# One-hot gate spreading with per-partition scalars, and expert low parts on one engine, in a one-core transformer layer

## The chip, the cores and the metric

The kernel runs on one core of a Trainium2 chip. The metric is device time in microseconds of one execution, median of several. Three runs of the kernel before took 3920.32, 3934.92 and 3938.32 us; its profiled execution took 3923.52 us.

## The reference

One layer of a latent-token backbone works on 512 tokens of width 2048: a mixer (state-space scan, pooling, gated merge, output projection), and then the part that the change touches, a product-key expert layer:

```
q = (h @ w_q) -> 8 heads, two halves of 128
s1, s2 = q half @ k1, k2                 # 128 scores each
top 16 of s1, top 16 of s2, top 16 of the 256 sums -> expert id = i1*128 + i2
g = softmax(top scores)                   # 128 (head, expert) pairs per token
act = gelu(h . u_tab[expert]) * g
out = sum over the pairs of act * v_tab[expert]     # 16384 experts of 2048
```

Afterwards comes the residual with a gate and a final normalization. All is float32.

## The kernel before

The expert layer begins after the mixers. It treats the first 128 tokens (tile 0) by gathering: for each of 128 (head, expert) pairs it fetches the rows of both tables by an indirect DMA from GpSimd (line 1081), takes the dot product on VectorE (line 1096), the gelu on ScalarE (1097, 1098), and adds the scaled row of the second table on VectorE (1089). The other 384 tokens (tiles 1 to 3) are done densely: `dense_u` multiplies them with the whole first table, `dense_v` with the whole second one, with the gates spread into a dense token-by-expert matrix.

TensorE reads float32 as a high and a low part, three products for one (lines 110 to 112). So each half MB of a table that is loaded (`wload`, line 124; 256 loads in `dense_u`, 256 in `dense_v`) is cast to its high part `whi` by ScalarE (125), and the low part `wlo = wraw - whi` is subtracted by VectorE or GpSimd (126). `lo_eng` deals these subtractions out: an accumulator grows by `lo_pool` = 0.5 at each load and gives the work to GpSimd whenever it reaches 1, so every other one. There are three buffers each for raw, high and low parts. `last_lo` is the latest subtraction recorded on VectorE.

Beside the loads run two lanes, stepped by `tick` in every `wload`: lane 0 is the gathering of tile 0 (0.29 pairs a load, later 0.25), lane 1 (1.1 steps a load) the preparation `prep`: `picks` turns the sorted keys of a tile into indices and softmax gates (lines 1043 to 1065, among them six VectorE operations over 128x2048), `dense_keys` transposes them so that the 128 pairs lie on the partitions, and `dense_gates` spreads them. For each group of four tokens, `dense_gates` makes one-hot matrices of the two key indices (line 1144, two operations), multiplies the second by the three bfloat16 pieces of the gate (1146, one operation over 3x4x128), and TensorE multiplies them (1152, twelve matmuls) into the gates of these tokens, which ScalarE copies out (1153). There are 96 such groups, so 192 steps of lane 1; they run between about 1725 and 2550 us.

A scheduler orders the instructions of each engine from its own estimate of times; subtractions and casts have a high priority. GpSimd's order is that of the code. `issue_after(last_lo)` queues the VectorE instructions of a block behind the last recorded subtraction; of the parts here only the gathering's are so bound. In `dense_v`, each four rows of gate products are multiplied by GpSimd (1199, `sr`), cast by ScalarE (135, `ah`) and subtracted on VectorE (136, `al`).

Of the kernel before, what the change touches and what calls it, by code (L numbers as in the profile page):

```python
# [6 lines left out]
F32 = mybir.dt.float32  # L7
F32R = mybir.dt.float32r
BF16 = mybir.dt.bfloat16
# [3 lines left out]
OP = mybir.AluOpType  # L13
# [4 lines left out]
P = 128  # L18
# [75 lines left out]
class Builder:  # L94
# [1018 lines left out]
    def dense_keys(self, t, res, ix):  # L1113

        nc, V, kp = self.nc, self.nc.vector, self.keep
        ps = self.psT.tile([P, 512], F32, tag="tr", name=self.nm("pst"))
        for j, x in enumerate(res[t]):
            nc.tensor.transpose(ps[:, j * P:(j + 1) * P], x, self.ident)
        iT = kp.tile([P, 2, P], BF16, name=self.nm("iT"))
        nc.scalar.copy(iT, ps[:, 0:2 * P].rearrange("p (j t) -> p j t", j=2))  # L1120
        wb = kp.tile([P, 3, P], BF16, name=self.nm("wb"))
        wf = self.tq.tile([P, P], F32, tag="wf", name=self.nm("wf"))
        r = self.tq.tile([P, P], F32, tag="wr", name=self.nm("wr"))
        V.tensor_copy(r, ps[:, 2 * P:3 * P])
        for q in range(3):
            V.tensor_copy(wb[:, q], r)
            if q < 2:
                V.tensor_copy(wf, wb[:, q])
                V.tensor_tensor(r, r, wf, op=OP.subtract)
        ix[t] = (iT, wb)  # L1130
        yield

    def dense_gates(self, ix):

        nc, V, NT = self.nc, self.nc.vector, 4
        for j, t in enumerate(DT):
            iT, wb = ix[t]
            for tg in range(P // TG):
                st = self.stp.tile([P, P, TG], F32, tag="ast", name=self.nm("ast"))
                for t4 in range(TG // NT):  # L1140
                    ts = slice(tg * TG + t4 * NT, tg * TG + t4 * NT + NT)
                    oh = self.ohp.tile([P, 2, NT, P], BF16, tag="oh", name=self.nm("oh"))
                    for q in range(2):
                        V.tensor_tensor(oh[:, q], self.io4, iT[:, q, ts].unsqueeze(2).broadcast_to([P, NT, P]), op=OP.is_equal)  # L1144
                    R = self.ohp.tile([P, 3, NT, P], BF16, tag="R", name=self.nm("R"))
                    V.tensor_tensor(R, oh[:, 1].unsqueeze(1).broadcast_to([P, 3, NT, P]),
                                    wb[:, :, ts].unsqueeze(3).broadcast_to([P, 3, NT, P]), op=OP.mult)
                    yield
                    ps = self.psT.tile([P, 512], F32, tag="tr", name=self.nm("psd"))
                    for n in range(NT):  # L1150
                        for q in range(3):
                            nc.tensor.matmul(ps[:, n * P:(n + 1) * P], oh[:, 0, n, :], R[:, q, n, :], start=(q == 0), stop=(q == 2))  # L1152
                    nc.scalar.copy(st[:, :, t4 * NT:t4 * NT + NT], ps.rearrange("p (t e) -> p e t", t=NT))
                    yield
                nc.scalar.dma_start(self.Gd[:, j * (P // TG) + tg], st)
# [103 lines left out]
    def peer(self):  # L1259
        tc, nc, I = self.tc, self.nc, self.I  # L1260
        pool = lambda **k: tc.tile_pool(**k)
        self.Sd = [self.dram.tile([P, NC, ND * P], F32, name=f"sd{c}") for c in range(P // NC)]
        self.Gd = self.dram.tile([P, ND * P // TG, P, TG], F32, name="gds")
        with self.es() as es:
            en = es.enter_context
            en(tc.manual_schedule(engines={mybir.EngineType.Pool}))
            ap = en(pool(name="ffn", bufs=1))
            acc0 = ap.tile([P, D], F32, name="ffn0")
            self.sm = sm = en(pool(name="sm3", bufs=4))
            es_k = self.es()  # L1270
            en = es_k.enter_context
            more = en(pool(name="wlo2", bufs=1))
            self.wlo = Turns([self.wlo, self.wlo, more])
            self.keep = en(pool(name="keep", bufs=1))
            self.rowp = en(pool(name="rows2", bufs=3))
            es_u = self.es()
            self.tq = es_u.enter_context(pool(name="tq", bufs=1))
            self.ohp = es_u.enter_context(pool(name="oh", bufs=2))
            self.io4 = self.tq.tile([P, 4, P], BF16, name="io4")
            nc.vector.tensor_copy(self.io4, self.iota.unsqueeze(1).broadcast_to([P, 4, P]))  # L1280
            res, ix = {}, {}

            def prep():
                yield from self.picks(self.tkp, 0, res)
                self.lane0[2].append(self.gather_tile(0, res, acc0))
                for t in DT:
                    yield from self.picks(self.tkp, t, res)
                    yield from self.dense_keys(t, res, ix)
                self.es_t.close()
                self.stp = es_u.enter_context(pool(name="ast", bufs=1))  # L1290
                yield from self.dense_gates(ix)

            self.lane0 = lane0 = self.lane(0.29, [])
            lane1 = self.lane(1.1, [prep()])
            self.lo_acc, self.lo_pool = 0.0, 0.5
            es_v = self.es()
            self.raw, self.A = {}, {}

            def late():
# [12 lines left out]
            for x in (self.ahp, self.alp):  # L1312
                x.pools += [pa] * 3
            op = es.enter_context(pool(name="outs", bufs=1, side="right"))
            outs = [op.tile([P, D], F32, name=f"ffn{t}") for t in DT]
            fp = es_v.enter_context(pool(name="fin", bufs=1))
            self.g2 = self.brow(fp, self.modd[:, 3 * D:4 * D], "g2b")
            self.fw = self.brow(fp, I["final_w"], "fwb")
            self.ss = [fp.tile([P, 4], F32, name=f"ssf{j}") for j in range(TT)]
            lane0[0], self.lo_pool = 0.25, 0.5  # L1320
            self.dense_v(outs)
            self.drain(lane0)
            es_v.close()
            es_k.close()
        self.hp.close()
# [70 lines left out]
```

## Time and profile before

| what | us or share |
|---|---|
| three runs | 3920.32, 3934.92, 3938.32 |
| profiled execution, and its span from first to last instruction | 3923.52, 3921.8 |
| granted TensorE clock over the span | 0.98 |
| busy: PE, DVE, ACT, POOL | 94%, 70%, 30%, 47% |
| `dense_u`: first and last matmul | 1593.1 to 2809.4 |
| `dense_v`: first and last matmul | about 2811 to 3904 |

PE is TensorE, DVE is VectorE, ACT is ScalarE, POOL is GpSimd. Matmuls are pipelined, so the duration of one is longer than the time from its start to the next one's start. Short VectorE instructions overlap in the same way: one starts before the end that is recorded for the one in front of it. The busy time of VectorE and GpSimd includes whatever holds an instruction up once it has started.

### The profile page before, as it was taken

The page shows a single profiled execution, that of the slowest core. Times are in us where ns is not written, and L with a number is a line of the kernel's source. Part 1 is how long each engine was busy: PE and PEld are TensorE (multiplying, and loading weights), DVE is VectorE, ACT ScalarE, POOL GpSimd, SP SyncE. Part 2 cuts the span into 40 slices and gives each one's busy share as a digit, 9 for nine tenths or more (in the row PEclk, how much of TensorE's full clock was granted, in tenths as well). Part 3 has the DMA queues.
Part 4 walks back from the last instruction along what each step waited for, and adds up shares of the span by engine and source line. Part 5 has one row for each costly group of instructions (what it writes and reads, how often), then busy time and mean ns, then how long its engine had stood idle before and what let it go on. Part 6 is the DMA issues. An engine that isn't in the chain of part 4 may idle for free. (4 is left out here: it accounts for less than half of the span.)

```text
span 3921.8 us, 49308 instructions
## 1 busy us (share of the span) xinstructions
PE 3686.4 (94%) x18841; PEld 3128.2 (80%) x18841; DVE 2732.1 (70%) x3331; ACT 1178.3 (30%) x1752; POOL 1834.7 (47%) x997
## 2 busy tenths in 40 slices
PE   5999998879899989899999999999999999999997
PEld 2478876657777868799999999999877878878886
DVE  4364369997473268999999999965666665666564
ACT  3223331112232232233333333333332333333232
POOL 0043115553223223355555655555565776676652
PEclk8999999999999999999999999999999999999999
DMA  8635658879876422378878878788887988888773
GB/s 263 213 118 182 213 165 231 225 218 289 245 235 199 135 75 91 105 248 285 299 282 300 301 286 300 278 300 296 320 301 258 321 298 286 304 298 298 273 278 120
DMA packets 456381, 954.40 MB, mean 243 GB/s; under 512 B 104720, under 2 KB 248464, under 8 KB 421072
## 3 DMA queue, kind: packets, MB, share of 16 engines
q1 hardware_dynamic: 380320, 584.58, 46.6%
q0 software_dynamic: 46464, 301.03, 21.0%
q10 hardware_dynamic: 29360, 65.64, 4.5%
q8 instruction: 147, 2.41, 0.2%
q14 instruction: 90, 0.74, 0.1%
HBM read 859.88 MB, written 94.93 MB: 243 GB/s over the span
## 5 line engine op out<-in xcount | busy, mean ns | idle before, releaser
L125 ACT CAST whi<-wraw 128x1024 fp32r<-128x1024 f32 x712 | 746.4, 1050 | 1724.9 <-PE psU L111 307.3
L126 POOL TENSOR_TENSOR wlo<-wraw,whi 128x1024 fp32r<-128x1024 f32 x284 | 792.5, 2791 | 803.6 <-ACT whi L125 591.6
L126 DVE TENSOR_TENSOR wlo<-wraw,whi 128x1024 fp32r<-128x1024 f32 x428 | 621.2, 1451 | 560.1 <-ACT whi L125 309.4
L112 PE MATMUL psU<-h2Th,wlo 128*128 128x384 f32 x2048 | 696.8, 340 | 42.5 <-DVE wlo L126 26.0
L110 PE MATMUL psU<-h2Th,whi 128*128 128x384 f32 x2048 | 702.0, 343 | 5.2 <-ACT whi L125 5.1
L111 PE MATMUL psU<-h2Tl,whi 128*128 128x384 f32 x2048 | 694.3, 339 | 0.0
L111 PE MATMUL psV<-wlo,ah 128*128 128x512 f32 x1536 | 607.0, 395 | 12.9 <-POOL wlo L126 7.1
L112 PE MATMUL psV<-whi,al 128*128 128x512 f32 x1536 | 605.9, 394 | 0.0
L110 PE MATMUL psV<-whi,ah 128*128 128x512 f32 x1536 | 556.1, 395 | 4.3 <-DVE ffn L1231 4.3
L112 PEld LDWEIGHTS psU<-h2Th,wlo 128*128 128x128 f32 x2048 | 388.8, 190 | 50.9 <-DVE wlo L126 19.3
L1096 DVE SCALAR_TENSOR_TENSOR row<-row,h 128x2048 f32<-128x2048 f32 x128 | 352.3, 2752 | 81.8 <-DMA row<-in_u,eid 81.7
L110 PEld LDWEIGHTS psU<-h2Th,whi 128*128 128x128 f32 x2048 | 388.6, 190 | 7.3 <-ACT whi L125 7.1
L111 PEld LDWEIGHTS psU<-h2Tl,whi 128*128 128x128 f32 x2048 | 389.0, 190 | 0.0
L1089 DVE SCALAR_TENSOR_TENSOR ffn<-row,w,ffn 128x2048 f32<-128x2048 f32 x127 | 351.3, 2766 | 18.0 <-DMA row<-in_v,eid 17.9
L111 PEld LDWEIGHTS psV<-wlo,ah 128*128 128x128 f32 x1536 | 290.1, 189 | 85.5 <-POOL wlo L126 11.7
L1081 POOL DMA_INDIRECT row<-in_u,eid x128 | 221.4, 1730 | 269.4 <-ACT w L1097 132.5
L110 PEld LDWEIGHTS psV<-whi,ah 128*128 128x128 f32 x1536 | 289.7, 189 | 71.1 <-issue 4.7
L112 PEld LDWEIGHTS psV<-whi,al 128*128 128x128 f32 x1536 | 289.5, 189 | 67.0
L1081 POOL DMA_INDIRECT row<-in_v,eid x128 | 277.0, 2164 | 20.0 <-issue 9.2
L819 DVE SCALAR_TENSOR_TENSOR lacc<-lw,sil,lacc 128x512 f32<-128x512 f32 x240 | 213.7, 891 | 58.6 <-DMA lw<-in_w_mod 56.5
L112 PE MATMUL psg<-hhi,wlo 128*128 128x512 f32 x512 | 203.1, 401 | 25.9 <-DVE wlo L126 25.8
L1144 DVE TENSOR_TENSOR oh<-io,iT 128x512 bf16<-128x512 bf16 x192 | 211.6, 1141 | 6.3 <-PE psd L1152 6.2
(349 smaller groups left out, 5567.4 us busy)
## 6 DMA issues: line engine op xcount, KB each, us to landing
wraw<-in_uT SPq DMA_DIRECT2D x256, 512.0 KB
wraw<-in_v SPq DMA_DIRECT2D x256, 512.0 KB
lw<-in_w_mod SPq DMA_DIRECT2D x256, 256.0 KB
wraw<-in_w_in SPq DMA_DIRECT2D x96, 512.0 KB
wmod<-in_w_mod SPq DMA_DIRECT2D x48, 512.0 KB
sd<-sev ACTq DMA_DIRECT2D x64, 384.0 KB
gds<-ast ACTq DMA_DIRECT2D x12, 2048.0 KB
sr<-sd SPq DMA_DIRECT2D x32, 768.0 KB
```

Of the source, the lines that this page charges most:

```text
L110: mm(ps, a.hi, b.hi, start=start, stop=False)
L111: mm(ps, a.hi, b.lo, start=False, stop=False)
L112: mm(ps, a.lo, b.hi, start=False, stop=stop)
L125: nc.scalar.copy(hi, raw)
L126: ins = (eng or nc.vector).tensor_tensor(lo, raw, hi.bitcast(F32), op=OP.subtract)
L819: nc.vector.scalar_tensor_tensor(acc, w, self.sil[:, k, 0:1], acc, op0=OP.mult, op1=OP.add)
L1081: nc.gpsimd.indirect_dma_start(out=r, out_offset=None, in_=I[tab], in_offset=bass.IndirectOffsetOnAxis(ap=eid[:, k:k + 1], axis=0))
L1089: V.scalar_tensor_tensor(acc, v, w, acc, op0=OP.mult, op1=OP.add)
L1096: V.scalar_tensor_tensor(u, u, 1.0, h2, op0=OP.mult, op1=OP.mult, accum_out=w[:, 0:1])
L1144: V.tensor_tensor(oh[:, q], self.io4, iT[:, q, ts].unsqueeze(2).broadcast_to([P, NT, P]), op=OP.is_equal)
```

## The change

It has three parts. First, the spreading of the gates: the two one-hot operations and the one product over all four tokens give way to sixteen `tensor_scalar` operations over 128x128, one for the first one-hot and three for the second one with the gate already multiplied, for each of the four tokens. The index and the gate piece of a token are one number in each partition. For that, indices and gate pieces stay in float32 (`iT`, `wp`); the matmuls and their operands are as before. Second, `lo_pool` is 0 in both expert stages, so that all 512 subtractions go to VectorE, and `last_lo` moves on with every load. Third, each step of `picks` is queued behind the latest subtraction.

```diff
-        iT = kp.tile([P, 2, P], BF16, name=self.nm("iT"))
+        iT = kp.tile([P, 2, P], F32, name=self.nm("iT"))
...
-        for q in range(3):
-            V.tensor_copy(wb[:, q], r)
-            if q < 2:
-                V.tensor_copy(wf, wb[:, q])
-                V.tensor_tensor(r, r, wf, op=OP.subtract)
+        V.tensor_copy(wp[:, 2], ps[:, 2 * P:3 * P])
+        for q in range(2):
+            V.tensor_copy(wb, wp[:, 2])
+            V.tensor_copy(wp[:, q], wb)
+            V.tensor_tensor(wp[:, 2], wp[:, 2], wp[:, q], op=OP.subtract)
...
-                    oh = self.ohp.tile([P, 2, NT, P], BF16, tag="oh", name=self.nm("oh"))
-                    for q in range(2):
-                        V.tensor_tensor(oh[:, q], self.io4, iT[:, q, ts].unsqueeze(2).broadcast_to([P, NT, P]), op=OP.is_equal)
+                    oh = self.ohp.tile([P, NT, P], BF16, tag="oh", name=self.nm("oh"))
                     R = self.ohp.tile([P, 3, NT, P], BF16, tag="R", name=self.nm("R"))
-                    V.tensor_tensor(R, oh[:, 1].unsqueeze(1).broadcast_to([P, 3, NT, P]),
-                                    wb[:, :, ts].unsqueeze(3).broadcast_to([P, 3, NT, P]), op=OP.mult)
+                    for n in range(NT):
+                        c = slice(ts.start + n, ts.start + n + 1)
+                        V.tensor_scalar(oh[:, n], self.iob, iT[:, 0, c], None, op0=OP.is_equal)
+                        for q in range(3):
+                            V.tensor_scalar(R[:, q, n], self.iob, iT[:, 1, c], wp[:, q, c], op0=OP.is_equal, op1=OP.mult)
...
+            def pinned(steps):
+                more = True
+                while more:
+                    with tc.issue_after(self.last_lo):
+                        more = next(steps, self) is not self
+                    yield
+
             def prep():
-                yield from self.picks(self.tkp, 0, res)
+                yield from pinned(self.picks(self.tkp, 0, res))
...
-            self.lo_acc, self.lo_pool = 0.0, 0.5
+            self.lo_acc, self.lo_pool = 0.0, 0.0
...
-            lane0[0], self.lo_pool = 0.25, 0.5
+            lane0[0] = 0.25
```

VectorE's queue in the middle of the gate spreading, before (`wlo` is a low part, `oh` the one-hots, `R` the product, `row` and `ffn` the gathering):

```order
L126 TENSOR_TENSOR wlo_16448<-wraw_16446,whi_16447 128x1024
L1146 TENSOR_TENSOR R_16455<-oh_16452,wb_13357 128x1536
L1144 TENSOR_TENSOR oh_16534<-io_12594,iT_13355 128x512 x2
L1146 TENSOR_TENSOR R_16537<-oh_16534,wb_13357 128x1536
L126 TENSOR_TENSOR wlo_16530<-wraw_16528,whi_16529 128x1024
L1096 SCALAR_TENSOR_TENSOR row_16398,w_16569<-row_16398,h_0_10626 128x2048
L1089 SCALAR_TENSOR_TENSOR ffn_12575<-row_16396,w_16391,ffn_12575 128x2048
L1144 TENSOR_TENSOR oh_16625<-io_12594,iT_13355 128x512 x2
L1146 TENSOR_TENSOR R_16628<-oh_16625,wb_13357 128x1536
```

The same queue, some loads away, now:

```order
L1144 TENSOR_SCALAR oh_18324<-iob,iT_13446 128x128
L1146 TENSOR_SCALAR R_18325<-iob,iT_13446,wp_13448 128x128 x3
L126 TENSOR_TENSOR wlo_18371<-wraw_18369,whi_18370 128x1024
L1096 SCALAR_TENSOR_TENSOR row_18211,w_18375<-row_18211,h_0_10626 128x2048
L1089 SCALAR_TENSOR_TENSOR ffn_12575<-row_18209,w_18204,ffn_12575 128x2048
L1144 TENSOR_SCALAR oh_18428<-iob,iT_13446 128x128
L1146 TENSOR_SCALAR R_18429<-iob,iT_13446,wp_13448 128x128 x3
L1144 TENSOR_SCALAR oh_18428<-iob,iT_13446 128x128
L1146 TENSOR_SCALAR R_18429<-iob,iT_13446,wp_13448 128x128 x3
L126 TENSOR_TENSOR wlo_18424<-wraw_18422,whi_18423 128x1024
```

There are twice as many low parts in it, and the pieces of one group can stand on both sides of a low part.

VectorE's queue at the start of `dense_u`, before, where the keys of the last head are still sorted (`oh`, `sel` and `iif` belong to the picks of tile 0, `den` and `gsm` to the softmax of several tiles):

```order
L1055 TENSOR_TENSOR oh_12611<-oh_12611,iif_12603 128x2048
L1063 TENSOR_REDUCE den_13029<-gsm_13026 128x8
L126 TENSOR_TENSOR wlo_12673<-wraw_12671,whi_12672 128x1024
L1057 TENSOR_REDUCE sel_12610<-oh_12611 128x128
L1064 RECIPROCAL den_13029<-den_13029 128x8
L1052 TENSOR_TENSOR oh_12708<-rf_12608,iota 128x2048
L1065 TENSOR_TENSOR gsm_13026<-gsm_13026,den_13029 128x128
L1055 TENSOR_TENSOR oh_12708<-oh_12708,iif_12603 128x2048
L1048 CAST rf_12850<-ri_12847 128x256
```

And now:

```order
L1055 TENSOR_TENSOR oh_12611<-oh_12611,iif_12603 128x2048
L126 TENSOR_TENSOR wlo_12673<-wraw_12671,whi_12672 128x1024
L1057 TENSOR_REDUCE sel_12610<-oh_12611 128x128
L1052 TENSOR_TENSOR oh_12708<-rf_12608,iota 128x2048
L1055 TENSOR_TENSOR oh_12708<-oh_12708,iif_12603 128x2048
L126 TENSOR_TENSOR wlo_12770<-wraw_12768,whi_12769 128x1024
L126 TENSOR_TENSOR wlo_12804<-wraw_12802,whi_12803 128x1024
L1060 TENSOR_TENSOR gsm_12808<-ts_10792 128x128
L1057 TENSOR_REDUCE sel_12610<-oh_12708 128x128
```

The work of later tiles has gone from this stretch, low parts that were GpSimd's stand in it, and `wlo_12673` comes behind the same operation of the picks as before.

## Rows read from the trace of the kernel before

**Rows 1.** Stretch 1725 to 2475: busy PE, weights, DVE, ACT, POOL; clock, DMA share, GB/s.
```profile
1725.00:2475.00 750.00, 738.21 (x4867) 719.66 (x4866) 718.28 (x489) 258.12 (x419) 433.52 (x172) 1.00 0.82 291
```

**Rows 2.** What PE waited for, 1593 to 1725 (sum, times, longest).
```profile
PE psU L112 <- DVE wlo L126: 16.8, 5, 12.3
PE psU L112 <- POOL wlo L126: 3.9, 1, 3.9
```

**Rows 3.** The same, 1725 to 2475.
```profile
PE psU L112 <- DVE wlo L126: 8.6, 9, 3.4
PE psU L112 <- POOL wlo L126: 3.1, 3, 1.9
```

**Rows 4.** The same, 2475 to 2811.
```profile
PE psU L112 <- POOL wlo L126: 9.3, 4, 3.4
```

**Rows 5.** The same, 2811 to 3904.
```profile
PE psV L111 <- POOL wlo L126: 7.1, 7, 1.7
PE psV L111 <- DVE wlo L126: 5.8, 3, 4.9
PE psV L110 <- DVE ffn L1231: 4.3, 1, 4.3
```

**Rows 6.** Busy time and granted clock (PEclk) after two stalls of PE.
```profile
1611.00:1635.00 24.00, 10.74 (x38) 10.13 (x39) 24.00 (x76) 3.57 (x6) 0.00 (x0) 0.64 0.16 44
1716.00:1720.00 4.00, 2.93 (x9) 2.94 (x10) 4.00 (x2) 0.00 (x0) 3.85 (x3) 0.60 0.84 290
```

**Rows 7.** PE's timeline around one group of gate matmuls (start, duration, instruction).
```profile
1999.78 0.34 PE L110 MATMUL psU<-h2Th,whi 128*128 128x384 f32 x1
...
2004.82 0.34 PE L112 MATMUL psU<-h2Th,wlo 128*128 128x384 f32 x1
...
2005.91 0.34 PE L111 MATMUL psU<-h2Tl,whi 128*128 128x384 f32 x1
```

**Rows 8.** VectorE by line, 1725 to 2475 (count, busy us, mean ns, idle before).
```profile
L1146 DVE TENSOR_TENSOR R<-oh,wb 128x1536 bf16<-128x1536 bf16 x85 | 181.7, 2137 | 1.4
L1144 DVE TENSOR_TENSOR oh<-io,iT 128x512 bf16<-128x512 bf16 x168 | 176.1, 1087 | 6.3 <-PE psd L1152 6.2
L1089 DVE SCALAR_TENSOR_TENSOR ffn<-row,w,ffn 128x2048 f32<-128x2048 f32 x47 | 131.6, 2801 | 0.0
L126 DVE TENSOR_TENSOR wlo<-wraw,whi 128x1024 fp32r<-128x1024 f32 x80 | 128.6, 1607 | 17.5 <-ACT whi L125 17.5
L1096 DVE SCALAR_TENSOR_TENSOR row<-row,h 128x2048 f32<-128x2048 f32 x47 | 115.7, 2462 | 6.3 <-DMA row<-in_u,eid 6.1
```

**Rows 9.** GpSimd by line, 1725 to 2475.
```profile
L126 POOL TENSOR_TENSOR wlo<-wraw,whi 128x1024 fp32r<-128x1024 f32 x79 | 233.4, 2955 | 147.8 <-ACT whi L125 130.8 <-PE psU L112 10.2 <-ACT w L1097 5.2
```

**Rows 10.** VectorE's timeline in `dense_v`.
```profile
3225.29 1.21 DVE L126 TENSOR_TENSOR wlo<-wraw,whi 128x1024 fp32r<-128x1024 f32 x1
3226.42 3.66 DVE L1233 TENSOR_TENSOR ffn<-ffn,psV 128x512 f32<-128x512 f32 x6
...
3236.00 2.34 DVE L1089 SCALAR_TENSOR_TENSOR ffn<-row,w,ffn 128x2048 f32<-128x2048 f32 x1
```

**Rows 11.** `tensor_scalar` by shape, whole span: two pointer scalars (L356), one (L338).
```profile
L356 DVE TENSOR_SCALAR hm<-hraw,modT 128x512 f32<-128x512 f32 x16 | 8.7, 542 | 0.1
...
L338 DVE TENSOR_SCALAR xt<-xt,rs 128x1024 f32<-128x1024 f32 x12 | 8.5, 747 | 0.1
...
L356 DVE TENSOR_SCALAR hm<-craw,modT 128x256 f32<-128x256 f32 x16 | 6.5, 407 | 0.0
```

**Rows 12.** Timeline: a VectorE dot product, a cast, and an indirect DMA on GpSimd.
```profile
1741.56 2.28 DVE L1096 SCALAR_TENSOR_TENSOR row<-row,h 128x2048 f32<-128x2048 f32 x1
1742.57 2.09 POOL L1081 DMA_INDIRECT row<-in_u,eid  x1 [0.30 <-issue]
...
1743.77 0.22 DVE L1126 CAST wb<-wr 128x128 bf16<-128x128 f32 x1
```

**Rows 13.** What VectorE waited for, 2811 to 3904.
```profile
DVE al L136 <- ACT ah L135: 146.9, 29, 7.3
```

More of the change, by code (lines that the diff above doesn't have):

```diff
@@ L1118, in dense_keys @@
             nc.tensor.transpose(ps[:, j * P:(j + 1) * P], x, self.ident)
-        iT = kp.tile([P, 2, P], BF16, name=self.nm("iT"))
+        iT = kp.tile([P, 2, P], F32, name=self.nm("iT"))
         nc.scalar.copy(iT, ps[:, 0:2 * P].rearrange("p (j t) -> p j t", j=2))
[L1121 to L1124, printed above, removed]
-        for q in range(3):
-            V.tensor_copy(wb[:, q], r)
-            if q < 2:
-                V.tensor_copy(wf, wb[:, q])
-                V.tensor_tensor(r, r, wf, op=OP.subtract)
-        ix[t] = (iT, wb)
+        wp = kp.tile([P, 3, P], F32, name=self.nm("wp"))
+        wb = self.tq.tile([P, P], BF16, tag="wb", name=self.nm("wb"))
+        V.tensor_copy(wp[:, 2], ps[:, 2 * P:3 * P])
[3 more added lines that the diff above has]
+            V.tensor_tensor(wp[:, 2], wp[:, 2], wp[:, q], op=OP.subtract)
+        ix[t] = (iT, wp)
         yield
@@ L1136, in dense_gates @@
         for j, t in enumerate(DT):
-            iT, wb = ix[t]
+            iT, wp = ix[t]
             for tg in range(P // TG):
@@ L1151, in dense_gates @@
                         for q in range(3):
-                            nc.tensor.matmul(ps[:, n * P:(n + 1) * P], oh[:, 0, n, :], R[:, q, n, :], start=(q == 0), stop=(q == 2))
+                            nc.tensor.matmul(ps[:, n * P:(n + 1) * P], oh[:, n, :], R[:, q, n, :], start=(q == 0), stop=(q == 2))
                     nc.scalar.copy(st[:, :, t4 * NT:t4 * NT + NT], ps.rearrange("p (t e) -> p e t", t=NT))
@@ L1278, in peer @@
             self.ohp = es_u.enter_context(pool(name="oh", bufs=2))
-            self.io4 = self.tq.tile([P, 4, P], BF16, name="io4")
-            nc.vector.tensor_copy(self.io4, self.iota.unsqueeze(1).broadcast_to([P, 4, P]))
+            self.iob = self.tq.tile([P, P], BF16, name="iob")
+            nc.vector.tensor_copy(self.iob, self.iota)
             res, ix = {}, {}
+            def pinned(steps):
[4 more added lines that the diff above has]
+                    yield
             def prep():
-                yield from self.picks(self.tkp, 0, res)
+                yield from pinned(self.picks(self.tkp, 0, res))
                 self.lane0[2].append(self.gather_tile(0, res, acc0))
                 for t in DT:
-                    yield from self.picks(self.tkp, t, res)
+                    yield from pinned(self.picks(self.tkp, t, res))
                     yield from self.dense_keys(t, res, ix)
```

## The prediction, made before the changed kernel ran

> **What bounds the kernel now.** I read the profile from the outside in: first the busy times in stretches, then what TensorE waits for in each, then the lines of VectorE and GpSimd, last single stretches of the timeline. In the expert stages, 1593 to 3904 us, TensorE is the engine that is nearly always busy: 738 of 750 us in the main stretch of the gate spreading [rows 1]. VectorE is busy 718 of the same 750, so the two are close to each other there, and which one is the bound has to be counted.
>
> TensorE's own need: 29 table matmuls start in 5.04 us, 0.1738 each, so a load (24 of them) takes 4.17. A group of gate matmuls adds 0.74: from 2004.82 to 2005.91 is 1.09, and two plain steps of 0.174 are in it [rows 7]. The stretch holds 80 + 79 = 159 loads and 85 groups [rows 8, 9], which is 663 + 63 = 726 us. It took 750. So 24 us are lost there; 11.7 of them have a name, waits for a low part from either engine [rows 3].
>
> In all, the named waits of TensorE are 20.7 us before 1725, 11.7 in the main stretch, 9.3 on GpSimd up to 2811, and 17.2 in `dense_v` [rows 2 to 5]. After a stall the clock is at its lower level for a while: 0.64 is granted on average over the 24 us after the first of them, and 0.60 over 4 us after one of 3.9 us [rows 6]. The first costs 0.36 x 24 = 8.6 us beside its waits, the second 1.6.
>
> VectorE's busy time is not all work. A low part that has the engine to itself takes 1.21 us [rows 10]; in the main stretch it takes 1.61 on average [rows 8], while GpSimd is at its own 79 low parts of 2.96 us [rows 9]. Dot products of 2.28 [rows 12] average 2.46, and the scaled sums of 2.34 [rows 10] average 2.80.
>
> The Trainium skill, in "SBUF — State Buffer", section "Who interferes with whom", says why: a VectorE instruction with two inputs from SBUF and a GpSimd one that reads SBUF exclude each other. The means above agree.
>
> **The low parts.** 256 subtractions leave GpSimd, 79 of them in the main stretch. VectorE gains as many at the pace of 1.13 us (3225.29 to 3226.42, the next one starts 0.08 before the recorded end [rows 10]). All 159 cost 180 us there. The gathering is 47 pairs at 2.21 (1741.56 to 1743.77 [rows 12]) and 2.34 less the 0.08 of overlap, so 4.47 together: 210 us, undisturbed now, as only GpSimd's DMA issues are left beside it. What the GpSimd engine had of low parts and TensorE waited for (3.9, 3.1, 9.3 and 7.1 [rows 2 to 5]) goes. VectorE is late next.
>
> **The one-hots.** A group was two one-hots of 1.09 and a product of 2.14 as they ran, 4.3 us [rows 8]. Now it is sixteen `tensor_scalar` over 128 elements: four with one pointer scalar, twelve with two. The trace has this operation in float32 with two pointers: 407 ns for 256 elements, 542 for 512 [rows 11], so 0.53 ns an element, and 339 for 128; less 0.08 of overlap, 0.26 us. With one pointer it is 747 for 1024, so 275 for 128, or 0.19. A group by these rows: 4 x 0.19 + 12 x 0.26 = 3.88 us. These operands are bfloat16, which no row has in this operation. Half the cost of an element would make 0.16 and 0.23, so 3.4; twice the cost, one element in about 1.05 ns as the other VectorE operations have it, 0.26 and 0.33, so 5.0. Below 3.4 it can't come, since most of the price is fixed for an instruction and shown. I take 3.6, between the nearest rows and their half. That is 306 us for the 85 groups; 289, 330 and 425 by the other prices.
>
> VectorE's sum in the main stretch is then 180 + 210 + 306 = 696 us against TensorE's 726: 96%, and 679, 720 and 815 by the other prices. It stays off the bound, by little. Since the new pieces are short and three buffers of low parts lie between the engines, most of the jitter is covered; I let a good half of the 11.7 us go, 6.
>
> The Trainium skill speaks against this part in "VectorE: DVE Perf Modes", section on the TRN2 errata: a fixed latency is paid by each instruction, so tiles of 512 elements and more are advised, and its table has 58 cycles plus the elements over the mode's rate. An estimate by that table at four elements a cycle is 94 ns, or 1.5 us a group; the rows, with the pointers in them, say over twice that. By the page the sum would be 518 us, VectorE far from the bound, and the time 18 us under the forecast, since all 24 would come back.
>
> **The picks behind the low parts.** They were ready early and stood in front of subtractions. But the longest stall of TensorE, 12.3 us [rows 2], is for `wlo_12673`, and in the new queue that one still stands behind the sorting of the last head and the same two picks of tile 0; about 2 us of other tiles' work have gone from in front of it and two low parts of 1.13 have come. I leave this stall and its 8.6 us of clock as they are. Of the rest before 1725 (4.5 and 3.9) I take 7.
>
> **The rest of `dense_u`, and `dense_v`.** After the gates, a load costs VectorE 1.13 + 0.29 x 4.47 = 2.4 of 4.17 us, so it has room; the 9.3 us go. In `dense_v` it is 1.13 + 0.25 x 4.47 and the `al` parts, under 3 of a load's 4.2; GpSimd's 7.1 go, and of the 5.8 some 2. The 4.3 behind the copying out of the accumulators stays [rows 5].
>
> **The sum.** 7 + 6 + 9 + 9 = 31 us of waits. The clock comes back with them: the stalls of 2 us and more that go are some five, at 1.6 each as after the one that rows show, 8 us. Together 39. The profiled execution took 3923.5, so 3884.5. Of the three runs the median is 11 above it, and I add a third of that: 3888.
>
> **Rivals.**
> - *VectorE and TensorE tie.* At 3.88 a group VectorE has 720 us to TensorE's 726, and nothing of the 24 comes back there; also part of the clock stays. 7 + 9 + 9 = 25, less 3 for new waits, makes 3902. For it: the nearest rows are these. Against it: bfloat16 is half as wide.
> - *The indirect DMAs hold up the new operations.* The Trainium skill has it in "SBUF — State Buffer", section "Who interferes with whom": such a `tensor_scalar` uses both port pairs and one of the two, it or GpSimd, blocks for the whole instruction of the other. Worked out from rows: the DMA that began at 1742.57 waited for the dot product to end at 1743.77 and took 0.89 more [rows 12]. There are 2 x 47 = 94 such in the stretch, 84 us. VectorE would have 780, 30 more than the stretch took, and 34 with the 11 groups outside it. Against 7 + 9 + 9 + 4 saved elsewhere that makes 3928, no change. Against it: the cast at 1743.77, one input and one output, ran beside those 0.89 us in 0.22.
> - *The new operations run at one element a step.* A group of 5.0 makes 815 us for VectorE, 65 more than the stretch took, 73 over all 96 groups. It decides from a group of 4.2 us, (750 - 390) / 85. Less 29 saved elsewhere: 3968, slower. Against it: the float32 rows are twice as fast as that.
> - *In `dense_v` every low part now stands in VectorE's queue behind `al`.* It waits 5.1 us on average, 29 times [rows 13], then runs 2.4, and a gathering pair of 4.5 can follow: 12.0 us, against the 12.5 that three buffers cover. Before, each second low part passed by on GpSimd. If 2.5 us of each reach TensorE, 72 are lost, and with 26 saved before it the time is 3970, slower. Against it: GpSimd's queue is empty of low parts, so that the product which `al` waits for starts earlier.
>
> **How the numbers follow.** Forecast 0.60, tie 0.14, DMA issues 0.09, one element a step 0.08, `al` 0.09. About 0.5% (20 us on the median of 3934.9) can be told from no change. The forecast is faster, and of the tie 0.09 too: 0.69. Its other 0.05 and the DMA issues are within 0.5%: 0.14. The two last are slower: 0.17. The forecast's own range is 3860 to 3905 (group prices of 3.4 to 3.88, none or all of the clock). The range that is given reaches 3855 to 3950, over the tie and the DMA issues, and leaves out the slower ones.
>
> **What would show it.** Low parts on VectorE at 1.2 us and no GpSimd row for them; `R` at 300 to 340 ns a piece with starts 0.23 to 0.26 apart; VectorE busy about 93 to 96% from 1725 to the last gate group; waits of TensorE for GpSimd gone, those for VectorE outside the first stall under 15 us; the 12 us stall near 1618 still there. I am wrong if starts of `R` lie over 0.29 apart, if TensorE waits for `R` or low parts by more than 25 us in the gate stretch, or if waits in `dense_v` grow.

## The result and the profile after

The changed kernel took 3904.03 us (median of seven runs, 3899.67 to 3914.49), the one before 3934.92 in the same comparison: a ratio of 0.9932, with a 95% interval of 0.9911 to 0.9953. It is faster, by 0.7% where 1.2% was forecast. The profiled executions stand at 3923.52 before and 3900.59 after, so 22.9 us apart where the sum had 39. From the first to the last matmul of each stage, `dense_u` went from 1216.3 us to 1190.9 (25.4 gained) and `dense_v` from 1091.5 to 1094.9 (3.4 lost). The rest is 0.9.

The main stretch after, busy times as in [rows 1]:

```profile
1725.00:2475.00 750.00, 744.85 (x4910) 724.50 (x4909) 697.90 (x1691) 266.88 (x427) 187.08 (x94) 1.00 0.80 295
```

TensorE has 6.6 us more of it, VectorE 20 us less, and GpSimd's 433 us have become 187. Its lines on VectorE, against [rows 8]:

```profile
L1146 DVE TENSOR_SCALAR R<-iob,iT,wp 128x128 bf16<-128x128 bf16 x1024 | 266.5, 327 | 0.0
L126 DVE TENSOR_TENSOR wlo<-wraw,whi 128x1024 fp32r<-128x1024 f32 x162 | 198.6, 1229 | 27.5 <-ACT whi L125 27.5
L1089 DVE SCALAR_TENSOR_TENSOR ffn<-row,w,ffn 128x2048 f32<-128x2048 f32 x47 | 110.7, 2355 | 0.0
L1096 DVE SCALAR_TENSOR_TENSOR row<-row,h 128x2048 f32<-128x2048 f32 x47 | 107.8, 2293 | 0.1
L1144 DVE TENSOR_SCALAR oh<-iob,iT 128x128 bf16<-128x128 bf16 x340 | 91.3, 269 | 24.5 <-PE psd L1151 24.5
```

Every operation that both kernels have is at its own pace again: the low part 1.23 us where it was 1.61, the scaled sum 2.36 where it was 2.80. VectorE's timeline in two groups, with one instruction of GpSimd, gives the price of the new pieces (start, duration, instruction, count):

```profile
2006.26 1.23 DVE L126 TENSOR_TENSOR wlo<-wraw,whi 128x1024 fp32r<-128x1024 f32 x1
2007.39 0.26 DVE L1144 TENSOR_SCALAR oh<-iob,iT 128x128 bf16<-128x128 bf16 x1
2007.56 0.77 DVE L1146 TENSOR_SCALAR R<-iob,iT,wp 128x128 bf16<-128x128 bf16 x3
2008.23 0.26 DVE L1144 TENSOR_SCALAR oh<-iob,iT 128x128 bf16<-128x128 bf16 x1
...
2016.33 0.27 DVE L1144 TENSOR_SCALAR oh<-iob,iT 128x128 bf16<-128x128 bf16 x1
2016.49 0.78 DVE L1146 TENSOR_SCALAR R<-iob,iT,wp 128x128 bf16<-128x128 bf16 x3
...
2016.72 0.95 POOL L1081 DMA_INDIRECT row<-in_v,eid  x1 [0.30 <-DVE oh L1144]
...
2017.16 0.27 DVE L1144 TENSOR_SCALAR oh<-iob,iT 128x128 bf16<-128x128 bf16 x1
```

A token takes 0.83 us from start to start (2007.39 to 2008.23, 2016.33 to 2017.16), so a group 3.33. A one-hot is 0.17 of it and each piece of `R` 0.22.

What TensorE waited for, by stage (sum, times, longest): 1593 to 1725, 1725 to 2475, 2475 to 2784 and 2784 to 3880, to be held against [rows 2 to 5].

```profile
PE psU L112 <- DVE wlo L126: 14.5, 2, 13.3
...
PE psU L110 <- ACT whi L125: 4.4, 2, 3.8
...
PE psU L110 <- ACT whi L125: 10.0, 1, 10.0
...
PE psV L111 <- DVE wlo L126: 7.0, 8, 1.6
PE psV L110 <- ACT ah L135: 6.2, 4, 2.0
PE psV L110 <- DVE ffn L1230: 3.3, 2, 2.4
PE psV L110 <- DVE ffn L1232: 2.6, 1, 2.6
```

All waits for GpSimd are gone. In their place stand one of 10 us for a cast near 2595, and in `dense_v` 6.2 us for `ah`, the high part of the gate products, which was no name on the list before. SyncE's queue and ScalarE around the first of these:

```profile
2576.81 0.33 SPq L1188 DMA_DIRECT2D sr<-sd  x1
2577.23 0.55 SPq L1189 DMA_DIRECT2D gr<-gds  x1
2577.82 2.21 SPq L1188 DMA_DIRECT2D sr<-sd  x1
2580.07 0.75 SPq L1189 DMA_DIRECT2D gr<-gds  x1
...
2582.75 1.05 ACT L125 CAST whi<-wraw 128x1024 fp32r<-128x1024 f32 x1 [2.72 <-PE psU L111]
...
2604.37 1.04 ACT L125 CAST whi<-wraw 128x1024 fp32r<-128x1024 f32 x1 [8.43 <-DMA wraw<-in_uT]
```

The first two pairs of scores and gates for `dense_v`, four transfers of 768 KB, are queued ahead of the next weight loads, and no cast runs for 21 us. The granted clock falls while TensorE waits, to 0.72 on average over the wait (first row), and is 0.50, the lower of its two levels (1.2 GHz), for 4.6 us behind it (second row). TensorE is busy for 4.35 of these, so an estimated 2 us are lost beside the wait:

```profile
2595.40:2605.50 10.10, 0.05 (x2) 0.03 (x1) 0.05 (x1) 1.53 (x2) 0.00 (x0) 0.72 0.90 318
2605.50:2610.10 4.60, 4.35 (x13) 3.84 (x14) 3.62 (x3) 2.10 (x2) 0.00 (x0) 0.50 0.48 135
```

### The profile page after: what moved, and what is told of

The parts are those of the page before. It is cut to its first block, busy times and chain, and to the rows that moved or that the text cites. A ratio compares the mean times of both kernels' runs of the same rounds, so it can differ in the third digit from the quotient of the medians.

```text
span 3898.8 us, 50589 instructions
## 1 busy us (share of the span) xinstructions
PE 3681.1 (94%) x18841; PEld 3124.1 (80%) x18841; DVE 2799.0 (72%) x4832; ACT 1188.6 (30%) x1758; POOL 1128.7 (29%) x741
## 4 chain that ended last, share of the span: by engine, by line
PE 48%; DMA 6%; DVE 5%; issue 2%; ACT 1%; POOL 1%; DVEq 0%; SPq 0%; ACTq 0%; POOLq 0%
PE psU L112 8%; PE psU L110 8%; PE psU L111 8%; PE psV L110 6%; PE psV L111 6%; PE psV L112 6%; DMA wraw<-in_v 4%; DVE wlo L126 2%; PE psd L1151 1%; PE psq L112 1%; PE psq L111 1%; PE psq L110 1%; DMA wraw<-in_uT 1%; ACT whi L125 1%; DVE ffn L1089 1%
## 5 line engine op out<-in xcount | busy, mean ns | idle before, releaser
L126 DVE TENSOR_TENSOR wlo<-wraw,whi 128x1024 fp32r<-128x1024 f32 x684 | 940.8, 1381 | 686.9 <-ACT whi L125 441.3
L1081 POOL DMA_INDIRECT row<-in_u,eid x128 | 350.7, 2740 | 1445.8 <-DVE row L1096 1333.6
L110 PE MATMUL psV<-whi,ah 128*128 128x512 f32 x1536 | 544.3, 396 | 12.9 <-ACT ah L135 6.2
L1146 DVE TENSOR_SCALAR R<-iob,iT,wp 128x128 bf16<-128x128 bf16 x1152 | 299.5, 328 | 0.0
L1089 DVE SCALAR_TENSOR_TENSOR ffn<-row,w,ffn 128x2048 f32<-128x2048 f32 x127 | 298.5, 2351 | 0.0
L1096 DVE SCALAR_TENSOR_TENSOR row<-row,h 128x2048 f32<-128x2048 f32 x128 | 292.8, 2288 | 4.0 <-DMA row<-in_u,eid 3.9
L110 PE MATMUL psg<-hhi,whi 128*128 128x512 f32 x512 | 205.1, 401 | 0.0
L111 PE MATMUL psg<-hlow,whi 128*128 128x512 f32 x512 | 204.4, 399 | 0.0
```

Of the source, the lines that this page charges most:

```text
L110: mm(ps, a.hi, b.hi, start=start, stop=False)
L111: mm(ps, a.hi, b.lo, start=False, stop=False)
L126: ins = (eng or nc.vector).tensor_tensor(lo, raw, hi.bitcast(F32), op=OP.subtract)
L1081: nc.gpsimd.indirect_dma_start(out=r, out_offset=None, in_=I[tab], in_offset=bass.IndirectOffsetOnAxis(ap=eid[:, k:k + 1], axis=0))
L1089: V.scalar_tensor_tensor(acc, v, w, acc, op0=OP.mult, op1=OP.add)
L1096: V.scalar_tensor_tensor(u, u, 1.0, h2, op0=OP.mult, op1=OP.mult, accum_out=w[:, 0:1])
```

## The experiments

Each is timed against the kernel before on the same chip; the kernel before had medians of 3926.0, 3930.6, 3921.8 and 3923.7 us in the four comparisons (the first four kernels below, the next four, then two and two).

**The low parts alone.** On the kernel before, with its one-hots and without the new pins:

```diff
-            self.lo_acc, self.lo_pool = 0.0, 0.5
+            self.lo_acc, self.lo_pool = 0.0, 0.0
...
-            lane0[0], self.lo_pool = 0.25, 0.5
+            lane0[0] = 0.25
```

> The kernel before with all low parts of both expert stages on VectorE and nothing else changed: gates spread by broadcast operations, picks not queued behind low parts. Theory (the gain comes from GpSimd's subtractions leaving the shared SBUF ports, and the one-hot form is of no weight): between 1725 and 2475 us VectorE needs 180 for low parts, 210 for the gathering and 85 x 2.9 = 245 for undisturbed gate groups, 635 of 750, less than the changed kernel; time 0.992 to 0.995 of before, 3900 to 3915 us, level with the changed kernel; the one-hot rows fall from 1.09 to about 0.68 us and the product from 2.14 to about 1.76. Rival (the one-hot form is what pays): with 256 more subtractions and the old form VectorE becomes the bound, no faster than before, 3930 us or more.

Measured: 3891.69 us (3887.93 to 3895.46), ratio 0.9912 (0.9894 to 0.993). The whole gain is here. VectorE in the main stretch:

```profile
L126 DVE TENSOR_TENSOR wlo<-wraw,whi 128x1024 fp32r<-128x1024 f32 x162 | 197.5, 1223 | 49.2 <-ACT whi L125 49.0
L1146 DVE TENSOR_TENSOR R<-oh,wb 128x1536 bf16<-128x1536 bf16 x88 | 154.0, 1751 | 0.2
L1144 DVE TENSOR_TENSOR oh<-io,iT 128x512 bf16<-128x512 bf16 x172 | 110.9, 686 | 40.5 <-PE psd L1152 40.4
L1089 DVE SCALAR_TENSOR_TENSOR ffn<-row,w,ffn 128x2048 f32<-128x2048 f32 x47 | 110.4, 2348 | 0.0
L1096 DVE SCALAR_TENSOR_TENSOR row<-row,h 128x2048 f32<-128x2048 f32 x47 | 107.4, 2285 | 0.3 <-DMA row<-in_u,eid 0.3
```

The old one-hots too were slow only beside GpSimd: 686 ns where [rows 8] have 1087, and 1751 where they have 2137. Left alone, a group of the old form costs 2.9 us of the queue, by its own timeline:

```profile
2052.01 1.29 DVE L1144 TENSOR_TENSOR oh<-io,iT 128x512 bf16<-128x512 bf16 x2
2053.21 1.27 DVE L126 TENSOR_TENSOR wlo<-wraw,whi 128x1024 fp32r<-128x1024 f32 x1
2054.41 1.74 DVE L1146 TENSOR_TENSOR R<-oh,wb 128x1536 bf16<-128x1536 bf16 x1
2056.07 1.21 DVE L126 TENSOR_TENSOR wlo<-wraw,whi 128x1024 fp32r<-128x1024 f32 x1
```

(2053.21 less 2052.01, and 2056.07 less 2054.41, make 1.20 + 1.66 = 2.86.) The new form at 3.33 is the dearer one.

**The one-hots alone**: the changed kernel without the pins, every other low part on GpSimd as before.

```diff
-            self.lo_acc, self.lo_pool = 0.0, 0.0
+            self.lo_acc, self.lo_pool = 0.0, 0.5
...
-                yield from pinned(self.picks(self.tkp, 0, res))
+                yield from self.picks(self.tkp, 0, res)
...
-                    yield from pinned(self.picks(self.tkp, t, res))
+                    yield from self.picks(self.tkp, t, res)
```

> The changed kernel with every other low part on GpSimd again in both stages, and the picks not queued: only the new form of the one-hots is left. Theory (as for the run before): the 79 subtractions of GpSimd in the gate stretch hold the ports, and the short operations wait behind them as the broadcasts did, up to 2.4 us for each; VectorE comes to 90 + 210 + 283 and up to 190 of waiting, 770 of 750; time 1.000 to 1.010 of before. Rival (the one-hot form pays): 0.993 to 0.996, like the changed kernel.

Measured: 3947.65 us (3945.49 to 3957.28), ratio 1.006 (1.004 to 1.008): slower. VectorE's lines of them in the main stretch:

```profile
L1146 DVE TENSOR_SCALAR R<-iob,iT,wp 128x128 bf16<-128x128 bf16 x976 | 350.7, 424 | 0.0
L1144 DVE TENSOR_SCALAR oh<-iob,iT 128x128 bf16<-128x128 bf16 x323 | 127.1, 393 | 0.2 <-PE psd L1151 0.2
```

Beside GpSimd's subtractions the small operations are held as the large ones were, 424 ns for 327 and 393 for 269. VectorE rose to 735.5 us of the 750.

**No pins on the picks.** The changed kernel with only the plain `self.picks(...)` lines of the diff just shown.

> The changed kernel without queueing the picks behind the low parts. Theory: the 12 to 13 us stall near 1618 is the sorting of the last head and the picks of tile 0, which the queueing does not move, so it stays and the time is within 5 us of the changed kernel (0.992 to 0.995 of before). Rival: the queueing holds the early low parts in place, and without it TensorE loses 10 us or more before 1725 (0.996 to 0.998).

Measured: 3901.21 us (3889.78 to 3905.53), ratio 0.9935 (0.9915 to 0.9956). The pins do nothing that can be measured. The stall near 1618 is 15.0 us without them and 13.3 with them.

**`dense_v` shared again.** The changed kernel with `lane0[0], self.lo_pool = 0.25, 0.5` before `dense_v`.

> The changed kernel with every other low part of the second expert stage (dense_v) on GpSimd again; dense_u as changed. The profile shows dense_v 3 us longer after the change, where 9 less were forecast. Theory (low parts on VectorE gain nothing there, since GpSimd's gate products still hold the ports and ScalarE's casts wait for them): dense_v back at 1091 to 1092 us, time within 5 us of the changed kernel, rather faster (0.991 to 0.993 of before). Rival (the forecast was right on dense_v and this profile an accident): 5 to 10 us slower than the changed kernel (0.995).

Measured: 3891.78 us (3886.75 to 3903.63), ratio 0.9919 (0.9898 to 0.994); `dense_v` takes 1087.4 us instead of 1094.9, and no wait for `ah` is left. So the low parts of that stage gained nothing on VectorE.

**The low parts of `dense_u` alone**, on the kernel before: the first hunk of the first diff without the second.

> The kernel before with one change: the low parts of dense_u all on VectorE, those of dense_v shared with GpSimd as before, old broadcast one-hots, nothing pinned. Theory A (the gain comes from dense_u's low parts alone, and VectorE with both stages' low parts loses in dense_v what it wins): dense_u as with the low parts of both stages on VectorE and the old one-hots (1187.7 us), dense_v as before or with the split restored (1087 to 1092), so 3888 to 3894, the same as that run (3891.7) within its interval. Rival B (the two runs with lower dense_v, 1087.6 and 1087.4, were lower for another reason, the gates' form): dense_v differs from both by more than 5 us and the total leaves 3885 to 3897.

Measured: 3892.58 us (3883.32 to 3895.95), ratio 0.9905 (0.9885 to 0.9924); `dense_u` 1183.9, `dense_v` 1088.5. This one line is the gain.

**The product of gates and scores on VectorE**, with the low parts of both stages there:

```diff
-        nc.gpsimd.tensor_tensor(sv, sv, gr, op=OP.mult)
+        nc.vector.tensor_tensor(sv, sv, gr, op=OP.mult)
```

> The kernel before with the low parts of both stages on VectorE and, besides, the product of the gates with the scores (sr by gr, 31 in dense_v, 3.5 us each on GpSimd) on VectorE as well; old one-hots, no pins. Theory A (in dense_v GpSimd's product holds the VectorE low part that runs beside it, 4.6 us where 1.2 us is its own time, and ScalarE's ah then comes late): the low parts of dense_v have a mean near 1.23 us instead of 1.57, the TensorE waits for ah (6 to 11 us in all) go, dense_v 1078 to 1083 us, total 3880 to 3888. Rival B (the waits for ah come from ScalarE's own queue or from the loads of sr and gr): the waits for ah stay within 2 us, dense_v stays 1086 to 1090, total 3889 to 3896. Rival C (a product of about 1.7 us on VectorE that waits for its loads blocks the low parts queued behind it): waits for wlo grow, dense_v above 1093.

Measured: 3922.29 us (3915.87 to 3930.43), ratio 0.9982 (0.9968 to 0.9996); `dense_v` took 1125.0 us. TensorE's waits in `dense_v`, and then VectorE's line of low parts:

```profile
PE psV L110 <- DVE ffn L1233: 20.0, 5, 4.0
...
PE psV L110 <- ACT ah L135: 1.4, 1, 1.4
```

```profile
L126 DVE TENSOR_TENSOR wlo<-wraw,whi 128x1024 fp32r<-128x1024 f32 x254 | 307.3, 1222 | 300.9 <-ACT whi L125 300.7
```

Half of what theory A said came true: the low parts are at 1.22 us and the waits for `ah` are nearly gone. The time went the way of rival C, though at another place than it named: the product of 1.75 us stands in front of the copying out of the accumulators, and TensorE waits 20 us for `ffn`.

**The second pair of loads later in the code**: `weights_load(1)` moved from `late()` to four expert columns further on, over the low parts on VectorE.

> The kernel before with the low parts of both stages on VectorE and, besides, the second pair of loads of scores and gates (sr, gr, 768 KB each) issued four expert columns later in dense_u instead of right behind the first pair. Theory A (the 10 us stall near 2595 in the changed kernel, 7.5 us near 2582 with the low parts alone, is there because 3 MB of these loads stand ahead of the weight loads on SyncE's queue): the stall falls to 0 to 4 us, the lower clock after it goes, dense_u 1178 to 1184, total 3880 to 3888. Rival B (the stall comes from the gather's transfers, or from the write of the gates that the first pair waits for): the stall stays 6 to 11 us, dense_u 1186 to 1191, total 3888 to 3896. Rival C: a second stall of equal size where the second pair now stands, total unchanged or longer.

Measured: 3891.73 us (3886.52 to 3897.23), ratio 0.991 (0.9891 to 0.993), with a stall of 7.2 us. It tells nothing apart: the scheduler put the second pair right behind the first again (2558.26 and 2559.23), so the order on the queue was that of the low parts alone.

**A subtraction on GpSimd that nobody waits for.** The low parts of both stages on VectorE, and once per expert column, behind a copy of one element that paces it:

```diff
+            if i2 < P - 9:
+                d = self.idle
+                nc.gpsimd.tensor_copy(d[:, 0:1], ev[:, i2 % 2, 0:1])
+                nc.gpsimd.tensor_tensor(d.bitcast(F32R), d, d, op=OP.subtract)
...
+            self.idle = self.tq.tile([P, 1024], F32, name="idle")
+            nc.gpsimd.memset(self.idle, 0.0)
```

> The kernel before with the low parts of both stages on VectorE and, besides, one subtraction of 128x1024 on GpSimd per expert column in dense_u (119 in all, about as many as GpSimd had before) whose result nobody reads; it adds work and no wait of TensorE. Theory A (GpSimd's subtractions cost VectorE its pace by holding the memory ports they share): the VectorE low parts in 1725 to 2475 go from 1.22 back to 1.5 to 1.7 us, TensorE's waits there grow by 15 to 30 us, dense_u 1203 to 1217, total 3905 to 3928. Rival B (TensorE had waited for GpSimd's own late low parts, 2.4 to 3.3 us each behind its DMA issues, and VectorE was not what limited): dense_u stays at 1186 to 1191 and the total at 3888 to 3896, though the low parts on VectorE are slower.

Measured: 4028.59 us (4020.16 to 4034.73), ratio 1.0258 (1.0234 to 1.0282), far beyond what theory A gave; `dense_u` took 1311.0. VectorE's and GpSimd's lines in the main stretch:

```profile
L126 DVE TENSOR_TENSOR wlo<-wraw,whi 128x1024 fp32r<-128x1024 f32 x148 | 223.3, 1512 | 4.8 <-ACT whi L125 4.8
L1146 DVE TENSOR_TENSOR R<-oh,wb 128x1536 bf16<-128x1536 bf16 x80 | 156.5, 1958 | 0.1
L1144 DVE TENSOR_TENSOR oh<-io,iT 128x512 bf16<-128x512 bf16 x156 | 142.5, 952 | 0.0
L1089 DVE SCALAR_TENSOR_TENSOR ffn<-row,w,ffn 128x2048 f32<-128x2048 f32 x42 | 104.6, 2492 | 19.2 <-DMA row<-in_v,eid 19.1
L1096 DVE SCALAR_TENSOR_TENSOR row<-row,h 128x2048 f32<-128x2048 f32 x43 | 101.8, 2369 | 15.5 <-DMA row<-in_u,eid 15.5
...
L1175 POOL TENSOR_TENSOR idle<-idle 128x1024 fp32r<-128x1024 f32 x74 | 218.6, 2954 | 6.0
```

Nobody reads the result of `idle`, and still each VectorE operation is longer than in the run with the low parts alone: by 289 ns, 207, 266, 144 and 84 in these rows. So it is the work on GpSimd itself that costs VectorE its pace, not a low part that comes late from it. That VectorE also kept all the low parts here makes the total worse than before: in `dense_u` TensorE waits 89.0 us for them, where it waits 18.3 with the low parts alone.

**The two pairs apart on the queue.** Low parts on VectorE, and the second pair pinned behind a later weight load:

```diff
-            nc.sync.dma_start(raw.rearrange("p (k n) -> p k n", k=kc), ap)
+            self.raws.append(nc.sync.dma_start(raw.rearrange("p (k n) -> p k n", k=kc), ap).ins)
...
-                self.weights_load(1)
+                with tc.issue_after(self.raws[-16]):
+                    self.weights_load(1)
```

> The kernel before with the low parts of both stages on VectorE and, besides, the second pair of loads of scores and gates pinned on SyncE's queue behind a later weight load: 15 weight loads now stand between the two pairs, which the run with the loads issued later in the code did not reach (there the scheduler left the two pairs together). Theory A (the stall of 7 to 10 us near 2580 to 2595 is there because two pairs, 3 MB, stand together ahead of the weight loads): with 1.5 MB at a time the stall is 0 to 4 us, the lower clock after it (6.8 us) mostly goes, dense_u 1176 to 1183 us, total 3879 to 3888. Rival B (one pair is enough to empty the three weight buffers, or the gathers' transfers are): a stall of 5 us or more stays, or a second one comes 60 to 70 us later, dense_u 1184 to 1191, total 3888 to 3897.

Measured: 3888.41 us (3886.59 to 3897.05), ratio 0.9921 (0.9904 to 0.9938). With the pairs 62 us and 15 weight loads apart (2558.83 and 2620.97) the stall of 7.5 us with the low parts alone is 1.6:

```profile
PE psU L110 <- ACT whi L125: 1.6, 1, 1.6
```

`dense_u` is at 1178.1, as theory A had it, where the low parts alone have 1187.7, so in that run the four transfers side by side are what made the stall. The total shows nothing of it: the ratio is 0.9921 where the low parts alone have 0.9912, and the time lies where rival B had it, at the lower end. In this profile `dense_v` is 1093.3, in that of the low parts alone 1087.6.

**Both moves together, on the old one-hots.** The pairs 8 weight loads apart, and the picking started six steps later, the first tile's behind the low parts:

```diff
             def prep():
+                for _ in range(6):
+                    yield
-                yield from self.picks(self.tkp, 0, res)
+                yield from pinned(self.picks(self.tkp, 0, res))
```

> The version that the runs so far point to: low parts of both stages on VectorE, old broadcast one-hots, the second pair of loads pinned some 8 weight loads behind the first, and the picking of keys started six steps later and queued behind the low parts (the changed kernel queues it too, but the stall of 13 to 15 us near 1618 stayed). Theory A (that stall is the low part of the second expert column waiting behind the picking, 13.7 us of VectorE work after its cast): with the picks later the low part follows the last of the top-16 selection, the stall falls to 5 to 9 us, and with the loads apart the total is 3870 to 3884. Rival B (the top-16 selection itself, which the pins do not reach, is what stands ahead of the low part): the stall stays 12 to 15 us; total 3880 to 3892 from the loads alone, or 3888 to 3896 if these do nothing either.

Measured: 3873.22 us (3871.59 to 3876.09), ratio 0.9875 (0.9857 to 0.9892), the fastest of all; its interval lies wholly below that of the changed kernel. The stall near 1618 is 7.3 us, and the main stretch is full:

```profile
1725.00:2475.00 750.00, 750.00 (x4966) 734.84 (x4965) 664.53 (x587) 264.85 (x429) 190.11 (x96) 1.00 0.82 298
```

**Both moves on the new one-hots**: the changed kernel with the last two diffs.

> The changed kernel, with its new one-hots and all its pins, and besides the two moves that gave 3873 us on the old one-hots: the second pair of loads apart from the first, and the picking of keys started six steps later. It differs from that version in the form of the one-hots and in the pins on three tiles' picks. Theory A (on a quiet GpSimd the new form costs VectorE 3.33 us a group against 2.88 for the old one, but VectorE is at 93% there and TensorE does not wait for it, so the form is worth nothing either way): ratio to before 0.985 to 0.990, 3863 to 3883. Rival B (38 us more of VectorE work in the gate stretch reach TensorE in part, as the 9 us between the changed kernel and the low parts alone suggest): ratio 0.990 to 0.993, waits of TensorE for VectorE or ScalarE in 1725 to 2475 of 5 us and more.

Measured: 3883.94 us (3881.41 to 3887.06), ratio 0.9895 (0.9874 to 0.9916): within theory A's ratios, and just past its times. Against the same moves on the old form the profile is 12.9 us longer: 7.0 in `dense_u` (1172.4 for 1165.4) and 7.2 in `dense_v`, which the form of the one-hots does not touch, less 1.1 before them. The intervals overlap, and in the main stretch TensorE waits only 2.4 us. That the new form costs something on a quiet GpSimd is likely; how much is open.

**The later picks alone**, with the pairs together:

> The kernel before with the low parts of both stages on VectorE and the picking of keys started six steps later, the first tile's queued behind the low parts; the two pairs of loads stand together as before. Theory A (the two moves of the version at 3873 us add up: the loads apart gave about 10 us in dense_u, the picks the rest): the stall near 1618 is 7 us instead of 13 to 15, the stall near 2580 to 2595 is 5 to 10 us, total 3876 to 3886. Rival B (the later picks alone gave all of it, since they also move the gates and with them where the loads fall): the stall near 2590 is under 3 us and the total 3870 to 3876.

Measured: 3879.37 us (3871.21 to 3884.21), ratio 0.9883 (0.9861 to 0.9906); stalls of 8.8 us near 1618 and 3.0 near 2594. `dense_u` is at 1170.4, where the low parts alone have 1187.7 and both moves together 1165.4. So in the profiles the picks gave most, and the second stall got smaller with them: the two moves don't simply add up. By the ratios neither step is clear of noise: this run's interval overlaps both that of the low parts alone and that of both moves. Only the two moves together lie clear of the low parts alone.

## Why the prediction was right, and where it was not

**VectorE's sum** held in size, and partly by luck: 696 us were forecast for the main stretch and 697.9 measured. The low part's pace is 1.13 as taken (2006.26 to 2007.39), but a group is 3.33 where 3.6 was taken, so the 85.3 groups need 284 us for the 306. Work that the sum left out fills the gap: 162 low parts for 159, 13.8 us of picks that stand in this stretch now (lines 1052, 1055 and 1057, 4.6 us each), and short operations. The 3.33 is also under the lower bound of 3.4, below which the prediction said it can't come. A piece of `R` is recorded at 327 ns on average, close to the 339 of the float32 rows, but the next one starts 0.10 us before its recorded end where 0.08 was taken. Whether the fixed part or the price of an element differs from float32 no run tells apart.

**The tie** stands at 3902, beside the measured 3904, and is not what happened. In the main stretch 162 loads of 4.17 and 85.3 groups of 0.74 are 739 us of TensorE's own need, so 11 are lost where 24 were: more came back than the 6 of the forecast. That the measured time lies at the tie's is chance.

**The step that failed first** is the one on `dense_v`: "GpSimd's 7.1 go, and of the 5.8 some 2". The 7.1 did go, and the named waits rose from 17.2 to 19.9 us: 7.0 for low parts, 6.2 for `ah`, 5.9 for the copying out of accumulators, 0.8 for a cast. Growing waits in `dense_v` were one of the signs that the prediction had named for being wrong. GpSimd has its product left, and a low part that runs beside it ends only 1.1 us after it (VectorE, ScalarE, GpSimd and TensorE near 3196):

```profile
3196.08 4.67 DVE L126 TENSOR_TENSOR wlo<-wraw,whi 128x1024 fp32r<-128x1024 f32 x1 [0.79 <-ACT whi L125]
3200.68 1.87 DVE L1232 TENSOR_TENSOR ffn<-ffn,psV 128x512 f32<-128x512 f32 x3
...
3199.90 1.47 ACT L135 CAST ah<-sr 128x1536 fp32r<-128x1536 f32 x1 [0.67 <-PE psV L111]
...
3196.14 3.52 POOL L1198 TENSOR_TENSOR sr<-sr,gr 128x1536 f32<-128x1536 f32 x1
...
3201.50 0.47 PE L110 MATMUL psV<-whi,ah 128*128 128x512 f32 x1 [1.44 <-ACT ah L135]
```

The prediction let GpSimd's low parts go and forgot that the product stays, now against every low part instead of every other. Nine profiles with all low parts on VectorE and the product on GpSimd have `dense_v` at 1087.6 to 1098.0 us (mean 1093.0), four with half of them on GpSimd at 1085.5 to 1091.5 (mean 1088.2). So the move is worth nothing there and probably costs some 5 us. Of the 254 low parts in the changed kernel's `dense_v`, the 42 that run beside a product average 3.32 us and the 212 others 1.22.

All four waits for `ah`, and two of the three for the copying out, end 1.8 us behind the end of a product. Two chains meet there: the held low part, with the copying out right behind it (3200.68), and the cast `ah`, which needs the product itself. Which of them comes last differs from run to run. In the nine profiles the waits for the copying out come to 5.9 to 11.0 us, in the four others to 0 to 4.4; those for `ah` are 0 to 2.8 in the other eight of the nine. So the 6.2 of the changed kernel's profile is not typical, and what grew with this move is mostly the copying out behind a held low part. That the `ah` waits come from the hold is not shown: taking the product away left 1.4 of them and put other waits in their place.

**The second** is "the 9.3 us go" between the gates and `dense_v`. GpSimd's waits went, and the loads of the first scores and gates made a stall of 10.0 us and its lower clock. The prediction did not look at SyncE's queue there. The same four transfers stand in the trace of before, with waits of 1.7 us at most near them; why they cost so little there is open. Of the 16 us between 3884.5 and 3900.6, 12 are in `dense_v` (3.4 lost for 9 gained) and 4 in `dense_u` (25.4 for its 22 of waits and most of the 8 of clock). In `dense_u` all of TensorE's waits went from 47.8 to 31.3 us, so 16.5 came back for the 22: the new stall outweighs what the main stretch gave beyond the forecast.

**The picks** were forecast right. The stall near 1618 stayed, 13.3 us for 12.3, and the waits for low parts before 1725 fell by 6.2 (20.7 to 14.5) for the 7 forecast. The pins have little part in it: the run without them has 16.3 there.

**The clock.** The prediction took 0.36 x 24 = 8.6 us as lost beside the first stall. The window of 24 us in [rows 6] holds the wait itself, and 4.7 of the 8.6 fall into it (0.38 x 12.3, first row), where TensorE had nothing to do. Behind the wait it worked at the lower level for 4.5 us (second row), so an estimated 2 us are lost there:

```profile
1618.20:1630.50 12.30, 0.01 (x1) 0.03 (x1) 12.30 (x38) 1.88 (x5) 0.00 (x0) 0.62 0.00 1
1630.50:1635.00 4.50, 4.50 (x14) 4.50 (x15) 4.50 (x4) 0.00 (x0) 0.00 (x0) 0.51 0.43 117
```

The 8.6 entered no term of the sum, since this stall was left as it is.

**The part that the sum did not separate.** It set the new one-hots, undisturbed, against the old ones as GpSimd held them, 3.6 for 4.3 us, and never worked out the old ones undisturbed. The trace of before had them: in the main stretch the median one-hot took 680 ns and the median product 1757, where the prediction took the means of 1087 and 2137. The means of [rows 8] less those of the low parts alone are 0.38 us on 80 low parts, 0.39 on 85 products, 0.40 on 168 one-hots, 0.45 on 47 scaled sums and 0.18 on 47 dot products: 160 us. Over GpSimd's 79 subtractions, VectorE lost 2.0 us for each low part that it was spared, and a low part costs it 1.13.

The Trainium skill, in "Perfetto Trace Analysis", section "Optimizing Scalar/DVE Operations", warns that moving work between these two might not help, since they share a port. By that rule the low parts should have been suspected first. The runs agree: giving every other one to GpSimd was a clear loss, 2.0 us for 1.13.

**The rivals.** The indirect DMAs did not hold the new pieces: the three at 2016.49 have the one of 2016.72 beside them and take 0.78 us, those at 2007.56 have none and take 0.77. All 337 pieces that overlap one average 348 ns, the 815 others 320, so they lose 28 ns each and 9 us in all, where the rival had 84 in the main stretch alone. The rival with one element a step had 0.33 us for a piece, and 0.22 refutes this price; what one element costs is not shown, since only one length ran. `al` no longer waits: 10.6 us in 12 waits for the 146.9 in 29 of [rows 13].

```profile
DVE al L136 <- ACT ah L135: 10.6, 12, 6.3
```

## What to carry to other kernels

Before work is split between VectorE and GpSimd, compare what the GpSimd instruction adds to VectorE's instructions beside it with what the work costs on VectorE: here 2.0 us against 1.13. Price both the old and the new form of a part under the conditions that the rest of the change will leave, since a part can look like a gain only because another part repairs what slowed the old one. When a stage gets faster, read the DMA queue of the stage behind it, and ask which instructions of another engine will still lengthen its own.

## What was not expected of the hardware

- A VectorE `tensor_scalar` over 128 bfloat16 elements started 0.17 us before the next instruction with one scalar from a pointer, and 0.22 with two.
- A low part of 1.22 us on VectorE took 3.32 on average beside GpSimd's product of 3.5 us.
- One GpSimd subtraction of 128x1024 that nobody reads, of 2.95 us, took VectorE about 1.5 us of pace: 111 us over 74 of them, by the differences of the means of five lines from those of the low parts alone. In the kernel before it was 2.0.
- With eight weight loads between two pairs of 768 KB transfers TensorE waited 0.6 us, with fifteen 1.6. Side by side they cost it 3.0 to 10.0 us in the runs with all low parts of `dense_u` on VectorE, and an estimated 2 of clock behind the longest; in the kernel before, 1.7 at most.
